# A decoder step on one core: closing one mLSTM head in a later list, opening the next in an earlier one

## Chip, cores and metric

One Trainium2 chip, one core of it. The metric is the device time of one execution in microseconds (us). Of the kernel before, three runs were timed: 988.92, 989.26 and 992.3; their median is 989.26.

## What is computed

One inference step of a two-layer decoder, in fp32, for one prompt of 512 tokens and eight samples of one new token each, which share the weights. Layer 0 is a sparse attention (compressed, selected and window branch), layer 1 an mLSTM with four heads of width 512; each mixer has one input and one output projection. The change touches the samples' part of the mLSTM. Per sample b and head, with T = 1, it is:

```
m_new = max(b + m, i);  decay = exp(b + m - m_new);  w = exp(i - m_new)
num = (q.k) w v + decay (q @ C);   den = (q.k) w + decay (q . n)
h = num / max(|den|, exp(-m_new)); h <- h * rsqrt(mean(h*h) + eps)
C <- decay C + w k v^T;            n <- decay n + w k
```

C is a 512 x 512 matrix per sample and head, 32 of them in all; each is read from HBM, used, updated and written back.

## The kernel before, in words

All tensors are laid out with features on the 128 partitions. A product in fp32 precision is made of three fp32r products: an operand x is split into xhi (a cast) and xlo = x - xhi, and hi*hi, hi*lo and lo*hi are added up in PSUM. So each weight tile is loaded by SP's DMA queue (wraw), cast by ScalarE or VectorE (whi) and subtracted by VectorE or GpSimd (wlo) before TensorE takes it.

The program is a series of seven lists of operations, numbered from 0, one after the other. A list says in which order its operations are issued; each engine takes its own operations of all lists strictly in that order. Lists 0, 1, 3 and 6 are recorded calls; lists 2, 4 and 5 are made with `P.op` and run with `P.run(ORDER, ...)` (class Plan, L485). `P.op` also notes an engine, a cost and a due time, but the class uses none of the three: the order is the tuple of operation numbers alone. ORDER1 (L108) is list 4, ORDER2 (L125) is list 5. MOVEDP1 and MOVEDP2 (L306, L310) name the operations whose first instruction goes to another engine than written (`swapped`, L651): an elementwise product, sum or difference changes between VectorE and GpSimd, a copy between ScalarE and VectorE. SLOTS (L318) gives, for each tile made, the buffer it takes; a tile waits until the last user of its buffer is done.

List 4 (L2366 to L2536) projects the 15 remaining gate columns (`zm_ops`: load, split, two chunks of 260 tokens of 24 matmuls each into mm, then zt = mm * rr, a sigmoid zsg in three ScalarE steps, the product zt * zsg, a small copy ZSS and a store zd), makes the prompt's gate rows (`gate_ops`; its last part transposes lse on TensorE and copies aT), and goes through the first sample head: state steps 0 to 7. It also issues the loads of the state tiles of steps 8 and 9.

List 5 (L2539 to L2969) is the prompt's mLSTM cell (`qk`, `v_split`, `values`), most of the output projection (`out_unit`), the samples' shares of it (`samples`) and state steps 8 to 31, that is sample heads 1 to 3. `qk` makes, per 128 features, two block diagonals bdm and bdk, the splits bh, bl of bdm and ch, cl of the input CT, and the q projection `f_po` from them.

The three pieces of a sample head:
- `head_open` (L2198). VectorE: `small`, five 128x32 products and sums into pr, wk and nT; `diag`, four copies that put q on the diagonal blocks of QZ1. TensorE: `rows`, four transposes of v. Then the split of these rows into VB, a copy (ScalarE) and a subtraction (VectorE).
- `state_step` (L2242), once per sample. TensorE: `run`, eight matmuls of two state tiles cs with QZ, kh = 1 first, into the bank d; `spread`, a broadcast of v by VB and OH. ScalarE scales the two cs tiles, VectorE adds the outer product to them, SP stores them. After the head's last step `keep` copies d to the tile ncs.
- `head_close` (L2294), a chain of nine: `small` (VectorE, tile sd), `sums` (TensorE, from ncs, sd and pr), `den` (VectorE, 3 small instructions), an absolute value (ScalarE), `num` (VectorE, 5, the last writes pr), `sq` (TensorE, from pr), `fac` (VectorE, 4), `root` (ScalarE, 2), `norm` (VectorE, 5, the last writes HN). HN of head 0 is next used by `samples` in the middle of list 5.

Before the change `state_step` calls `head_open` ahead of its head's first step and `head_close` after its last, so head 0 is opened and closed in list 4, and head 1 opened in list 5:

```
        if b == 0:                              # L2245
            head_open(P, hd, due - 8)
        ...
        if b == 7:                              # L2291
            head_close(P, hd, due + 3)
```

At the seam of the lists the orders before are, engine by engine. TensorE: last gate projection, `sq` of head 0, gate transposes; list 5: `rows` of head 1, `run` of steps 8 and 9, q projections 0 and 1, the spreads of steps 8 and 9, ... VectorE: last zt = mm * rr, `num` of head 0, last zt * zsg, `fac`, `norm`; list 5: `diag` of head 1, block diagonal 0, ... ScalarE: last sigmoid, `root`, aT; then the constant onesr; list 5: ch, ...

Of the kernel before, what the change touches and what calls it, by code (L numbers as in the profile page):

```python
# [123 lines left out]
)  # L124
ORDER2 = (  # L125
# [46 lines left out]
)  # L172
# [541 lines left out]
def step_kernel(ctx, tc, ap):  # L714
# [1527 lines left out]
    def state_step(P, k, due):  # L2242
        hd, b = divmod(k, 8)
        qz = QZ1[hd % 2]
        if b == 0:  # L2245
            head_open(P, hd, due - 8)
# [885 lines left out]
```

## Time and profile before

| | |
|---|---|
| median of three timed runs | 989.26 us (988.92 to 992.3) |
| the profiled execution, its own time | 989.0 us |
| its span, first to last instruction | 987.3 us |
| instructions | 22906 |
| mean granted TensorE clock | 0.998 of full speed |
| list 4 in the trace | from about 589 to 707 us |
| list 5 in the trace | from about 707 to 962 us |

The profile is one execution; a busy engine counts from an instruction's start to its end. Matmuls overlap in the pipeline, so from one to the next goes less time than one lasts. PE is TensorE's matmul, PEld its weight load, DVE VectorE, ACT ScalarE, POOL GpSimd, SP the queue that issues nearly all DMAs. Nearly every instruction is recorded through one helper, so rows are told apart by tile names, out<-in, and not by their line (L677).

### The profile page before, as it was taken

How to read it: one execution, taken by the hardware profiler on the slowest of the kernel's cores; microseconds unless marked ns; L12 is line 12 of the kernel's file. 1: busy time of each engine (PE TensorE's matmuls, PEld its weight loads, DVE VectorE, ACT ScalarE, POOL GpSimd, SP SyncE). 2: the span in 40 equal slices, each digit the busy share in tenths (PEclk: the TensorE clock that was granted, in tenths of full speed). 3: DMA queues.
4: the chain of work that ended last, by engine and by line, in shares of the span. 5: the costliest groups of instructions: out<-in, count | busy, mean ns of one | idle time of the engine just before them, and what ended most of it. 6: DMA issues, size and time to landing. Idle time of an engine off the chain costs nothing. (4 is left out here: it accounts for less than half of the span.)

```text
span 987.3 us, 22906 instructions
## 1 busy us (share of the span) xinstructions
PE 966.8 (98%) x8393; PEld 868.4 (88%) x8393; DVE 810.3 (82%) x1968; ACT 568.2 (58%) x1260; POOL 342.3 (35%) x418
## 2 busy tenths in 40 slices
PE   7999999999999999999999999999899999999998
PEld 5799999899988878799999997999788788778997
DVE  7988986776489988856777897966689999999986
ACT  6746443423488788633336655656687763755533
POOL 1123434421233344632133224232354633334340
PEclk9999999999999999999999999999999999999999
DMA  8755632324435434545644364887889899878643
GB/s 297 242 167 188 200 122 67 127 97 141 138 120 160 129 109 153 181 165 181 212 154 134 134 218 164 270 310 264 289 294 317 277 330 317 277 277 305 208 135 119
DMA packets 123683, 197.21 MB, mean 200 GB/s; under 512 B 16166, under 2 KB 64551, under 8 KB 123315
## 3 DMA queue, kind: packets, MB, share of 16 engines
q1 hardware_dynamic: 117954, 185.39, 57.1%
q10 hardware_dynamic: 5616, 10.36, 2.8%
q8 instruction: 66, 1.08, 0.4%
q14 instruction: 47, 0.38, 0.1%
HBM read 145.99 MB, written 58.10 MB: 207 GB/s over the span
## 5 line engine op out<-in xcount | busy, mean ns | idle before, releaser
L677 PE MATMUL mm<-hhi,whi 128*128 128x260 f32 x928 | 266.4, 287 | 0.2 <-DVE whi L677 0.2
L677 PE MATMUL mm<-hhi,wlo 128*128 128x260 f32 x928 | 262.4, 283 | 1.4 <-DVE wlo L677 1.3
L677 PE MATMUL mm<-hlo,whi 128*128 128x260 f32 x928 | 262.0, 282 | 0.0
L677 PEld LDWEIGHTS mm<-hhi,whi 128*128 128x128 f32 x928 | 174.7, 188 | 3.2 <-PE d L677 0.8
L677 PEld LDWEIGHTS mm<-hhi,wlo 128*128 128x128 f32 x928 | 174.8, 188 | 2.1 <-DVE wlo L677 2.0
L677 PEld LDWEIGHTS mm<-hlo,whi 128*128 128x128 f32 x928 | 174.7, 188 | 1.1 <-issue 0.5
L677 POOL TENSOR_TENSOR wlo<-wraw,whi 128x512 fp32r<-128x512 f32 (+1 forms) x35 | 64.4, 1842 | 121.9 <-DVE whi L677 43.1
L677 DVE SCALAR_TENSOR_TENSOR cs<-t,wk,cs 128x512 f32<-128x512 f32 x128 | 88.7, 742 | 11.2 <-ACT cs L677 10.4
L677 DVE TENSOR_TENSOR wlo<-wraw,whi 128x1024 fp32r<-128x1024 f32 (+1 forms) x64 | 73.9, 1155 | 10.4 <-ACT whi L677 6.5
L677 ACT ACTIVATE cs<-cs,SBC 128x1024 f32<-128x1024 f32 x64 | 71.3, 1146 | 12.5 <-PE d L677 10.4
L677 ACT ACTIVATE s<-s,mn 128x256 f32<-128x256 f32 (+3 forms) x128 | 70.6, 555 | 7.6 <-DVE mn L677 4.9
L677 ACT ACTIVATE whi<-wraw 128x1024 fp32r<-128x1024 f32 (+1 forms) x59 | 51.2, 871 | 41.1 <-PE mm L677 26.7
L677 POOL TENSOR_SCALAR s<-s,sm 128x256 f32<-128x256 f32 (+3 forms) x53 | 50.6, 965 | 53.9 <-DVE sm L677 27.1
L677 PE MATMUL mm<-uh,whi 128*128 128x260 f32 x224 | 65.0, 290 | 1.8 <-DVE kwl L677 1.8
L677 PE MATMUL mm<-uh,wlo 128*128 128x260 f32 x224 | 63.6, 284 | 0.3 <-POOL wlo L677 0.3
L677 PE MATMUL mm<-ul,whi 128*128 128x260 f32 x224 | 63.3, 283 | 0.3 <-DVE ul L677 0.3
L677 DVE CUSTOM_DVE_ANT_0 s<-s,D 128x128 f32<-128x128 f32 (+3 forms) x128 | 58.3, 485 | 5.5 <-PE s L677 4.1
L677 PE MATMUL s<-phi,w1a 128*128 128x256 f32 (+1 forms) x224 | 49.1, 297 | 0.0
L677 PE MATMUL mm<-uo,whi 128*128 128x260 f32 x256 | 46.2, 283 | 0.0
L677 PEld LDWEIGHTS mm<-uh,whi 128*128 128x128 f32 x224 | 42.1, 188 | 3.8 <-DVE kwl L677 2.0
L677 DVE TENSOR_TENSOR plo<-praw,phi 128x256 fp32r<-128x256 f32 (+1 forms) x50 | 39.1, 792 | 7.1 <-ACT phi L677 4.0
L677 PEld LDWEIGHTS mm<-ul,whi 128*128 128x128 f32 x224 | 42.2, 188 | 1.3 <-issue 0.5
(526 smaller groups left out, 2648.1 us busy)
## 6 DMA issues: line engine op xcount, KB each, us to landing
cs<-in_state_C SPq DMA_DIRECT2D x64, 512.0 KB, 5.5
o_cs<-cs SPq DMA_DIRECT2D x64, 512.0 KB, 5.0
praw<-in_cache SPq DMA_DIRECT2D x128, 128.0 KB, 3.1
dk<-in_cache SPq DMA_DIRECT2D x128, 128.0 KB, 2.6
wraw<-in_m_in SPq DMA_DIRECT2D x32, 512.0 KB, 4.2
wraw<-in_m_out SPq DMA_DIRECT2D x32, 256.0 KB, 4.6
wraw<-in_w_kv SPq DMA_DIRECT2D x11, 512.0 KB, 5.0
wraw<-in_w_q SPq DMA_DIRECT2D x8, 512.0 KB, 3.3
```

Source lines behind the costliest of these rows:

```text
L677: return f(*[real(x) for x in a], **{n: real(x) for n, x in k.items()})
```

## The change

Head 0 is closed in list 5 instead of list 4 (its operations are now the first that list 5 makes), and head 1 is opened in list 4 instead of list 5. List 4 has 344 operations instead of 348, list 5 has 1033 instead of 1029. No operation is added or dropped in total, and none of the moved ones issues a DMA. ORDER1 and ORDER2 are new throughout, and so are MOVEDP1, MOVEDP2 and the buffers in SLOTS from list 4 on. The code, and the first of the two swap lists:

```diff
@@ -304,16 +305,16 @@
     850, 855, 860, 870, 899, 906, 916, 920, 921, 922, 923, 924, 927, 928, 929, 930, 933,
 )
 MOVEDP1 = (
-    1, 12, 16, 22, 27, 31, 32, 46, 57, 61, 62, 72, 77, 82, 87, 91, 92, 102, 107, 112, 117, 121, 132, 136, 137, 142,
-    147, 151, 166, 172, 177, 182, 187, 192, 196, 197, 202, 212, 225, 230, 244, 248, 255, 328,
+    1, 12, 16, 17, 32, 42, 46, 47, 62, 77, 87, 91, 92, 97, 102, 117, 121, 127, 136, 151, 157, 162, 166, 177, 181,
+    182, 192, 196, 197, 202, 222, 225, 230, 342,
 )
 MOVEDP2 = (
-    75, 82, 170, 265, 272, 287, 288, 291, 292, 294, 309, 313, 325, 327, 328, 330, 331, 348, 349, 351, 353, 371, 376,
-    386, 401, 413, 423, 425, 426, 427, 433, 436, 438, 443, 451, 454, 459, 475, 476, 477, 483, 490, 493, 494, 495,
-    501, 515, 520, 525, 537, 545, 556, 557, 561, 565, 571, 575, 576, 579, 583, 585, 600, 601, 605, 609, 616, 618,
-    619, 621, 623, 631, 634, 637, 642, 666, 691, 699, 707, 725, 731, 741, 748, 772, 774, 776, 778, 781, 784, 786,
-    793, 794, 795, 808, 811, 813, 814, 817, 823, 824, 826, 828, 835, 838, 845, 851, 858, 864, 865, 871, 879, 900,
-    920, 925, 926, 933, 937, 941, 951, 959, 977, 999, 1006, 1020,
+    79, 86, 174, 269, 276, 287, 289, 291, 293, 295, 307, 313, 314, 321, 331, 335, 349, 350, 352, 353, 355, 361, 366,
+    367, 375, 379, 380, 385, 390, 397, 421, 431, 432, 433, 434, 436, 439, 458, 463, 476, 478, 487, 493, 497, 499,
+    510, 519, 524, 534, 561, 565, 571, 572, 574, 577, 578, 580, 581, 586, 587, 589, 592, 595, 601, 602, 605, 607,
+    619, 620, 623, 625, 627, 637, 640, 641, 643, 646, 649, 671, 695, 703, 711, 719, 729, 730, 734, 752, 760, 771,
+    774, 785, 786, 787, 790, 792, 794, 797, 798, 799, 802, 806, 815, 828, 839, 840, 842, 844, 845, 849, 855, 861,
+    862, 869, 882, 889, 903, 904, 929, 937, 945, 955, 963, 1003, 1010, 1024,
 )
 SLOTS = {
     ("wstream", "w"): (
@@ -2242,7 +2243,7 @@
     def state_step(P, k, due):
         hd, b = divmod(k, 8)
         qz = QZ1[hd % 2]
-        if b == 0:
+        if b == 0 and hd != 1:
             head_open(P, hd, due - 8)
         for n in (2 * k, 2 * k + 1):
             if ("cs", n) not in D:
@@ -2533,6 +2534,7 @@
     for n in range(2 * NZ, 2 * NZ + 4):
         state_load(P, n, ZT * 15 - 10)
         D["cs", n].users.append(-1)
+    head_open(P, 1, ZT * 15 - 8)
     P.run(ORDER1, R, NE, MOVEDP1)
     r1.close()
     wctx.close()
@@ -2946,6 +2948,9 @@
     P = Plan({**CAPS, "bdk": 5, "bdm": 2, "ctw": 2, "qf": 2, "qh": 2, "ql": 2, "ch": 2, "cl": 2, "bh": 2, "bl": 2, "kwh": 1, "kwl": 1, "cpt": 2, "wb": 1, "zs": 1, "ab": 1, "wt": 2,
               "Sh": 1, "Sl": 1, "acc": 1, "sq1": 1, "hx": 1, "hy": 1, "fraw": FWB[0], "fhi": FWB[1], "flo": FWB[2]},
              held + CTI + sum(VTI, []), KEPT)
+    for n in (("nc", 0), ("pr", 0), ("pr", 1), ("wk", 1)):
+        D[n] = Tile_(n[0])
+    head_close(P, 0, 0)
     for k in range(NZ, 32):
         state_step(P, k, CS0 + CSP * (k - NZ))
     v_split(P, 0, 0)
...
```

The orders at the seam after the change, engine by engine (a star: on the other engine by the swap lists):
- TensorE, list 4: `rows` of head 1 between the projections of column 12; at the end the last gate projection, gate transposes. List 5: `sums` of head 0, spreads of steps 8 and 9, q projection 0, `run` of steps 8 and 9, q projections 1 and 2, the scores of tiles 0 and 1, q projection 3, the scores of tile 2, `sq` of head 0, `run` of step 10, ...
- VectorE, list 4: `diag` of head 1 before the first zt of column 13, VB by two instructions behind it; at the end the first zt of column 15, the second gate product of column 14, `keep` of head 0, the last zt = mm * rr, aT. List 5: block diagonals 3* and 1*, `small` of head 0, block diagonals 0* and 2*, cl 0, bl 0, bl 1, `den`, cl 1, `num`, ...; `fac` some 30 and `norm` some 70 VectorE operations later.
- ScalarE, list 4: last sigmoid. Then onesr; list 5: ch 0, bh 1, bh 0, ch 1, ...
- GpSimd, list 4: the gate product of column 15, first chunk, ZSS 14, the product of its second chunk*, ZSS 15.
- SP, list 4: store of the second tile of step 7, of the first of step 7, zd 14, load of the state tile 16 (step 8, kh = 0; before it was loaded earlier and tile 17 late), zd 15. List 5: load of tile 21, wb, load of tile 20, ab, ...

What the swap lists move, counted by kind over the whole of each list (operations, before to after):

| list 5 | written for, runs on | before | after |
|---|---|---|---|
| 512-wide differences (cl, vl, ul, wlo), products (num * zs), sums (acc) | GpSimd, on VectorE | 18 | 19 |
| the same | VectorE, on GpSimd | 28 | 24 |
| Sl (128 to 512 wide) | VectorE, on GpSimd | 9 | 8 |
| block diagonals bdm, bdk (128 wide) | GpSimd, on VectorE | 12 | 16 |
| bl (128 wide) | VectorE, on GpSimd | 11 | 10 |
| casts out of SBUF (ch, vh, whi, Sh, uh) | ScalarE, on VectorE | 16 | 19 |
| copies out of PSUM, 512 wide (qh, kwh, cpt) | ScalarE, on VectorE | 8 | 10 |
| copies, 128 wide (bh, qf) | ScalarE, on VectorE | 15 | 11 |
| nP, 4 wide | VectorE, on ScalarE | 1 | 3 |

| list 4 | written for, runs on | before | after |
|---|---|---|---|
| wlo, 1024 wide | VectorE, on GpSimd | 3 | 1 |
| wlo, 1024 wide | GpSimd, on VectorE | 6 | 7 |
| gate products, 260 wide | VectorE, on GpSimd | 16 | 12 |
| gate products, 260 wide | GpSimd, on VectorE | 2 | 1 |
| whi, 1024 wide | ScalarE, on VectorE | 11 | 10 |
| `keep`, aT and one tensor_scalar of rows | VectorE, on ScalarE or GpSimd | 3 | 0 |

## Rows read from the trace of the kernel before

**Rows 1.** The page, part 1: each engine's busy time in us, its share of the span, its instructions.
```profile
PE 966.8 (98%) x8393; PEld 868.4 (88%) x8393; DVE 810.3 (82%) x1968; ACT 568.2 (58%) x1260; POOL 342.3 (35%) x418
```

**Rows 2.** Busy time of each engine by stretch (list 4; list 5 but for its first 18 and last 12 us; its last 12). The columns are the stretch and its length, then PE, PEld, DVE, ACT and POOL busy in us with the number of instructions, the granted clock, the DMA share and GB/s.
```profile
589.00:707.00 118.00, 115.92 (x1054) 104.22 (x1052) 85.81 (x192) 71.77 (x165) 40.51 (x63) 1.00 0.75 253
...
725.00:950.00 225.00, 222.31 (x1734) 186.84 (x1733) 211.22 (x455) 135.26 (x240) 93.33 (x104) 1.00 0.86 291
950.00:962.00 12.00, 11.72 (x98) 11.51 (x97) 9.16 (x17) 5.03 (x11) 7.50 (x8) 1.00 0.01 3
```

**Rows 3.** Waits of TensorE over the whole span: what it waited for, us in total, times, the longest.
```profile
PE d L677 <- DVE QZ L677: 2.0, 1, 2.0
PE mm L677 <- DVE kwl L677: 1.8, 1, 1.8
...
PE t L677 <- DVE pr L677: 1.3, 1, 1.3
```

**Rows 4.** The same view as rows 2, in stretches of 2 us behind the seam.
```profile
708.00:710.00 2.00, 1.58 (x9) 0.71 (x13) 1.97 (x9) 2.00 (x5) 0.00 (x0) 0.68 1.05 405
710.00:712.00 2.00, 2.00 (x13) 0.34 (x5) 1.94 (x8) 1.17 (x3) 0.51 (x2) 0.50 0.99 192
```

**Rows 5.** Timeline of TensorE: start, duration, operation, out<-in, shapes, count of the merged instructions, and in brackets the idle time before and what ended it. First `sums` of head 0 in list 4, then the seam.
```profile
691.46 0.44 PE L677 MATMUL t<-sd,ncs 128*32 128x8 f32 x32
691.73 0.32 PE L677 MATMUL t<-pr,ones 128*32 128x64 f32 x8
...
703.48 0.28 PE L677 MATMUL mm<-hhi,wlo 128*128 128x260 f32 x1
705.10 0.27 PE L677 MATMUL t<-pr,ones 128*32 128x32 f32 x8 [1.33 <-DVE pr L677]
705.29 0.66 PE L677 MATMUL t<-cst,lse 128*128 128x128 f32 x4
705.79 0.60 PE L677 MATMUL t<-cst,VS 128*8 128x128 f32 x4
708.42 3.53 PE L677 MATMUL d<-cs,QZ 128*32 128x512 f32 x16 [2.03 <-DVE QZ L677]
711.88 0.61 PE L677 MATMUL mm<-ch,bh 128*128 128x512 f32 x1
...
712.79 0.40 PE L677 MATMUL mm<-ch,bh 128*128 128x512 f32 x1
...
713.49 0.62 PE L677 MATMUL t<-VB,OH 128*128 128x512 f32 x2
...
716.53 1.07 PE L677 MATMUL d<-cs,QZ 128*32 128x512 f32 x8
```

**Rows 6.** Timeline of VectorE at the seam.
```profile
701.50 0.42 DVE L677 TENSOR_TENSOR zt<-mm,rr 128x260 f32<-128x260 f32 x1
703.80 0.43 DVE L677 TENSOR_TENSOR zt<-mm,rr 128x260 f32<-128x260 f32 x1 [1.88 <-PE mm L677]
...
707.94 0.19 DVE L677 TENSOR_TENSOR HN<-nm,dn 128x32 f32<-128x32 f32 x1
708.05 0.39 DVE L677 COPY QZ<-QKS 128x8 f32<-128x8 f32 x4
```

**Rows 7.** Timeline of ScalarE at the seam.
```profile
704.71 0.87 ACT L677 ACTIVATE zsg<-zsg 128x260 f32<-128x260 f32 x2
...
707.08 0.30 ACT L677 ACTIVATE onesr<-ones 128x128 fp32r<-128x128 f32 x1
707.27 1.66 ACT L677 ACTIVATE ch<-CT 128x512 fp32r<-128x512 f32 x3
```

**Rows 8.** Timeline of SP's DMA issues before the seam.
```profile
701.64 0.33 SPq L677 DMA_DIRECT2D zd<-zt  x1
702.02 1.56 SPq L677 DMA_DIRECT2D cs<-in_state_C  x1
```

**Rows 9.** The tile view of cs over the whole span, its last line, for the loads and stores of 512 KB each.
```profile
DMA to landing us min/median/max: 3.0/5.3/9.7
```

**Rows 10.** Groups of instructions by line, engine and form between 707 and 962 us: count, busy us and mean ns of one, then the idle time before them. The first is GpSimd's, the others VectorE's.
```profile
L677 POOL TENSOR_TENSOR vl<-VT,vh 128x512 fp32r<-128x512 f32 x11 | 14.7, 1340 | 19.0 <-PE mm L677 10.8 <-DVE vh L677 6.3 <-ACT vh L677 1.9
...
L677 DVE TENSOR_TENSOR vl<-VT,vh 128x512 fp32r<-128x512 f32 x5 | 3.4, 680 | 0.0
L677 DVE CAST kwh<-t 128x512 fp32r<-128x512 f32 x5 | 3.4, 680 | 0.0
...
L677 DVE CAST vh<-VT 128x512 fp32r<-128x512 f32 x4 | 2.1, 537 | 0.0
...
L677 DVE TENSOR_TENSOR bdm<-cst,mw 128x128 f32<-128x128 f32 x5 | 1.6, 324 | 0.0
```

**Rows 11.** Timeline of all engines from 845 to 850 us.
```profile
845.92 2.53 POOL L677 TENSOR_TENSOR num<-num,zs 128x512 f32<-128x512 f32 x2
...
846.02 1.23 DVE L677 SCALAR_TENSOR_TENSOR hf_v<-rs_t,rs_y 128x8 f32<-128x8 f32 x1
...
847.28 1.19 DVE L677 TENSOR_TENSOR dn<-hf_v,dn 128x8 f32<-128x8 f32 x1
...
849.36 0.39 PE L677 MATMUL mm<-uh,whi 128*128 128x260 f32 x1 [1.78 <-DVE kwl L677]
```

**Rows 12.** The tile view of hf_v, one of the small instructions of `norm`: count, then min, median and max duration in ns.
```profile
L677 DVE SCALAR_TENSOR_TENSOR hf_v<-rs_t,rs_y x4: 166/168/1229, 707.5 to 943.1; 128x8 f32<-128x8 f32 x4
```

More of the change, by code (lines that the diff above doesn't have):

```diff
@@ L420 @@
     ("st0", "cse"): (
-        0, 1, 2, 2, 1, 0, 1, 2, 0, 1, 2, 0, 1, 0, 2, 1, 0, 2, 1, 2, 0, 2, 1, 0, 2, 1, 0, 2,
+        0, 1, 2, 1, 2, 0, 0, 1, 2, 1, 0, 2, 1, 2, 0, 2, 0, 1, 2, 0, 1, 1, 0, 2, 0, 2, 1, 0,
     ),
@@ L429 @@
     ("zp", "zsg1"): (
-        0, 1, 1, 0, 1, 0, 1, 0, 1, 0, 0, 1, 0, 1, 0, 1, 0, 1, 0, 1, 1, 0, 1, 0, 0, 1, 1, 0, 1, 0, 1, 0,
+        0, 1, 1, 0, 1, 0, 1, 0, 1, 0, 1, 0, 1, 1, 0, 1, 0, 1, 1, 0, 1, 0, 0, 1, 1, 0, 1, 0, 1, 0, 1, 0,
     ),
     ("st", "cs"): (
-        0, 1, 2, 3, 0, 1, 2, 3, 2, 1, 0, 3, 1, 0, 2, 3, 0, 2, 3, 1, 0, 3, 1, 2, 0, 3, 2, 1, 0, 2, 3, 1, 2, 0, 3, 1,
+        0, 1, 2, 3, 2, 0, 1, 3, 0, 2, 1, 3, 2, 0, 1, 3, 2, 0, 3, 1, 1, 2, 3, 0, 2, 1, 3, 0, 1, 2, 3, 0, 3, 1, 2, 0,
     ),
@@ L440 @@
     ),
[4 rows of a table added]
+    ),
     ("cella", "row"): (
[4 rows of a table removed]
-    ),
[4 rows of a table removed]
[4 rows of a table added]
+    ),
+    ("cellb", "row"): (
+        0, 1, 2, 3, 4, 5, 3, 1, 2, 0, 1, 5, 2, 3, 4, 3, 1, 5, 2, 0, 2, 3, 5, 1, 2, 4, 5, 1, 0, 3, 5, 4, 0, 1, 2, 3,
+        5, 0, 4, 1,
     ),
     ("fw", "w"): (
-        0, 1, 2, 3, 4, 5, 1, 0, 2, 3, 4, 1, 0, 5, 2, 4, 3, 1, 0, 2, 5, 4, 3, 0, 1, 3, 2, 5, 1, 0, 4, 5, 1, 2, 3, 1,
-        0, 4, 5, 2, 1, 0, 3, 2, 5, 4, 0, 3, 1, 2, 4, 5, 3, 0, 1, 4, 2, 5, 0, 3, 1, 2, 5, 4, 0, 1, 3, 4, 5, 2, 0, 3,
-        1, 2, 4, 5, 3, 0,
-    ),
-    ("cellb", "row"): (
-        0, 1, 2, 3, 4, 5, 3, 0, 2, 1, 5, 4, 0, 3, 2, 0, 4, 3, 1, 5, 3, 4, 1, 2, 3, 5, 0, 4, 1, 2, 0, 4, 1, 5, 3, 0,
-        4, 1, 2, 5,
+        0, 1, 2, 3, 4, 5, 0, 3, 4, 0, 2, 1, 5, 2, 4, 3, 1, 5, 4, 2, 0, 3, 1, 4, 3, 5, 2, 3, 4, 1, 5, 0, 2, 1, 4, 2,
+        1, 0, 4, 2, 5, 3, 1, 4, 2, 0, 2, 3, 1, 2, 0, 5, 2, 1, 4, 3, 0, 1, 5, 2, 4, 0, 1, 3, 5, 4, 2, 0, 3, 1, 5, 2,
+        4, 0, 1, 3, 5, 2,
     ),
@@ L2290, in state_step @@
             P.op("SP", 0.4, due + 5 - kh, store, r=[half[kh]], mb=0.524)
-        if b == 7:
+        if b == 7 and hd:
             head_close(P, hd, due + 3)
```

165 rows, old and new, of tables (ORDER1, ORDER2, SLOTS) are left out of this document.

## The prediction, as it was put on record

> **What bounds the kernel now.** I read the page first. TensorE is busy 98% of the span and VectorE 82% [rows 1], so a change that adds and removes no matmul can only win where TensorE waits or runs slow. Then the stages, cut at the starts of lists 4 and 5: list 4 holds 2.1 us of TensorE waiting in 118, list 5 holds 2.7 in its 225 main us and 0.3 in its last 12 [rows 2]. VectorE is busy 211.2 of those 225: it is nearly a second bound there, with 13.8 us to spare. Then who was waited for: the three longest single waits outside the start of the program are for QZ (2.0), kwl (1.8) and pr (1.3), all VectorE's [rows 3]. QZ and pr lie side by side at the seam of the two lists. There the granted clock also falls to 0.68 and 0.50 [rows 4], that is to the lower level, 1.2 GHz.
>
> **The seam before, step by step** [rows 5]. Call z the end of list 4's last projection matmul, 703.48 + 0.28 = 703.76. TensorE then has the first head's closing sums of squares (start 705.10), gate transposes (705.29), the second head's opening transposes (705.79), two state steps (708.42) and list 5's first q projection (711.88, the next starts 712.79). Undisturbed these take 0.2 + 0.5 + 0.6 + 2.1 (twice the 1.07 of the step at 716.53) + 0.7 (713.49 - 712.79) = 4.1. They took 712.79 - 703.76 = 9.0, so 4.9 was lost: 1.3 waiting for pr, 2.0 for QZ, 1.5 at the lower clock. The cause is VectorE's order. pr is a link of the closing's chain, and the opening's copies into QZ (708.05) are queued behind the chain's last link at 707.94, though they need nothing of it [rows 6]. ScalarE is held too: its first work for list 5 starts at 707.08, though the last sigmoid ended at 704.71 + 0.87 = 705.6; the closing's root stands between [rows 7].
>
> **What the change does there.** Opening the second head in list 4 makes QZ, the transposes and VB ready before z: TensorE's 0.6 of transposes goes before z, beside projections it would do anyway, and VectorE's part (about 2 us) lies in list 4, where VectorE idles 118 - 85.8 = 32 us [rows 2]. Neither step issues a DMA. After z TensorE's new order is: gate transposes, closing sums, two spreads, q projection, two state steps.
> - The sums need sd, behind the last zt product, the aT copy and two block diagonals on VectorE. The product ends at z + 0.5 (703.80 + 0.43 [rows 6]); 0.2 + 2 x 0.32 + 0.2 [rows 10, 12] put sd at z + 1.5. The transposes end at z + 0.5, so TensorE waits 1.0. This is the wait that replaces the one for pr.
> - Sums 0.6 (691.46 to 691.73 + 0.32), spreads 0.5: z + 2.6 [rows 5].
> - The projection needs ch, cl, bh, bl. ScalarE: last sigmoid to z + 1.8, onesr, ch at z + 2.0 to 2.6 [rows 7]; VectorE: cl 0.7 (as the vl subtraction [rows 10]), bl 0.2, ready at z + 3.5. TensorE waits 0.9 more, then projects to z + 4.2 and steps to z + 6.3.
> Lost: 1.9 instead of 4.9, if the clock holds. I take it that it does: the wait of 1.78 before 849.36 [rows 11] falls in a stretch that stayed at the full clock [rows 2], and the two new waits are 1.0 and 0.9 with matmuls between. Gain: **3.0**. Bounds: no more than 4.9; at worst the clock falls all the same (1.5) and the state tile of step 8 lands late. That load is now the last of list 4 on SP's queue, behind a zd store that waits for a gate product placed after the product of 701.50. That product ends at z - 1.8 [rows 6], the gate product some 0.4 later, and SP issues the load 0.4 behind the store [rows 8]: at about z - 1.0. Loads of this kind land after 3.0 / 5.3 / 9.7 us (least, median, most) [rows 9], this one then at z + 2.0 / 4.3 / 8.7, and step 8 needs it for its second half at z + 4.7: nothing lost at the median, 4.0 at the most. So the seam gives between -2.5 and +4.9.
>
> **The rest of list 5.** I counted, per kind, the operations that the two swap lists move, after minus before. From GpSimd to VectorE: five 512-wide subtractions or products (0.68 [rows 10]), one narrower (at most 0.68), five 128-wide (0.32): 5.7 us. From ScalarE: three net casts out of SBUF (0.54), two out of PSUM (0.68), less four 128-wide (at most 0.32) and two tiny ones: 1.4. The closing brings 18 small instructions of 0.17 [rows 12], 3.1; the opening takes away 1.9. VectorE has **about 8 us more** in list 5; GpSimd has at least 6 x 1.34 = 8.0 less [rows 10]. The 8 lie beside TensorE's work as long as the 13.8 of VectorE's idle time covers them; without that cover they would be TensorE's waits.
> Against this stands what GpSimd costs VectorE: two closing instructions of 0.17 took 1.23 and 1.19 while GpSimd ran two products (845.92, 2.53), and TensorE's wait of 1.78 for kwl is queued behind them [rows 11, 12].
> The trace has no row for the new order. From both sides: the change can return no more than the 2.7 + 0.3 that TensorE waits there [rows 2], and loses no more than all 8 us. I take **+0.7**: that one wait of 1.8 needs a coincidence of GpSimd and a chain, likelier gone than not with GpSimd relieved, while other small waits will come up with VectorE at 97%.
>
> **A rule on the pages.** The row shows small VectorE instructions of two inputs held for about as long as a GpSimd product lasts [rows 11]. The Trainium skill, GPSIMD Engine Reference, Specifications, says that GpSimd shares its SBUF interfaces with VectorE and contends with its instructions of two SBUF inputs or in a two-port mode. The trace agrees with that. It speaks against moving the closing into list 5. As a mechanism here: GpSimd's busy share rises from 40.5/118 to 93.3/225 around the moved chain [rows 2], and a chain held as at 846 costs 2.1 us of VectorE more. With the 8 that makes 10, still under 13.8, so the sum stays and rival C gets a larger chance.
>
> **The sum.** 3.0 + 0.7 = 3.7 off the profiled execution's 989.0 (span 987.3 and 1.7 around it) gives 985.3; the median of the runs shown stands 0.3 higher: **985.6**. List 4's other moves I cost at nothing: some 6 us more for VectorE, covered by its 32 idle.
>
> **Rivals.**
> A, everything goes: the seam as worked out or better, and list 5's waits vanish. For: those waits are few and one place holds most of them; against: VectorE gets fuller. 989.3 - 3.0 - 3.0 = 983.3, at best 989.3 - 4.9 - 3.0 = 981.4. Chance 0.25.
> B, the gap only changes its owner: the state tile lands late and the clock falls, 4.0 + 1.5 more than I forecast: 989.3 - 3.0 + 5.5 = 991.8. It decides from a landing later than 5.7 us after issue. For: the range of landings; against: the median. Chance 0.15.
> C, the other side: VectorE becomes list 5's bound. Place: 725 to 950; price: the 8 us, or 10 with held chains; it decides when VectorE's added work exceeds what its idle time, spread as it lies, can take. 989.3 - 3.0 + 8 = 994.3, up to 996.3. For: 94% busy already; against: 13.8 idle and less GpSimd. Chance 0.10.
> That the change doesn't do what it says (VectorE held as often as before) lies in the forecast's lower edge: 986.3 without the 0.7.
>
> **Numbers.** The forecast's own case, 984 to 988, has 0.50. A measurement here can tell about 0.5%, 4.9 us: below 984.3 is faster, above 994.2 slower. Faster: nearly all of A and a fifth of the forecast, 0.34. Slower: half of C and the tail of B, 0.07. Same: 0.59. Range 982.0 to 991.5: it leaves out A's best, the costlier half of B, and C.
>
> **What would show it.** Right: no wait for QZ or pr at the seam; one wait near 1.0 for sd or nc before the closing sums and one below 1 for the first projection; full clock from 700 to 715; state steps 8 and 9 done by z + 6.5; VectorE's busy time in list 5 up by some 8, GpSimd's down by as much. Wrong: a wait for a DMA of cs at the seam (B), VectorE without idle time and TensorE waiting for ql, kwl or bl through list 5 (C), or the lower clock still granted there.

## The result, and the profile after

The changed kernel takes **984.18 us** (median of 5 runs, 983.27 to 984.77) against 989.53 (5 runs) beside it: a ratio of 0.9941, 95% interval 0.9929 to 0.9952, so 5.3 us or 0.6% less. 985.6 was forecast, with a range of 982.0 to 991.5. The profiled execution took 984.77, its span is 983.0.

The page's first line after [rows 1]: VectorE is a little busier (810.3 to 812.5), GpSimd less (342.3 to 326.0), TensorE the same within 0.7.

```profile
PE 966.1 (98%) x8393; PEld 868.3 (88%) x8393; DVE 812.5 (83%) x1986; ACT 568.0 (58%) x1260; POOL 326.0 (33%) x400
```

The gain is found by cutting both traces at three events of TensorE: the first state step of list 4, z (the start of list 4's last projection matmul plus 0.28), the first score product (`s<-qh,ch`), and the first matmul of the closing phase (`s<-uh,whi`). Below I call the stretches list 4, the seam and the rest. Stage windows, columns as in [rows 2]; the kernel before:

```profile
604.80:703.76 98.96, 98.96 (x841) 91.69 (x840) 70.75 (x123) 59.92 (x116) 32.27 (x43) 1.00 0.80 272
703.76:714.64 10.88, 7.51 (x44) 4.11 (x44) 8.03 (x35) 7.39 (x18) 2.60 (x6) 0.84 0.98 303
714.64:947.44 232.80, 230.11 (x1778) 193.09 (x1777) 218.87 (x473) 145.61 (x259) 97.05 (x111) 1.00 0.86 289
```

and the changed kernel:

```profile
605.75:704.78 99.03, 99.00 (x807) 91.64 (x807) 76.40 (x137) 61.06 (x116) 19.83 (x33) 1.00 0.79 277
704.78:712.12 7.34, 6.03 (x72) 3.14 (x70) 6.04 (x23) 6.71 (x17) 2.68 (x7) 1.00 0.67 201
712.12:943.24 231.12, 230.27 (x1786) 193.13 (x1785) 219.06 (x487) 144.93 (x260) 91.78 (x100) 1.00 0.87 294
```

List 4 takes the same (98.96, 99.03). The **seam** goes from 10.88 to 7.34, 3.5 less, though it now holds 72 matmuls instead of 44 (the closing's first sums came in; the opening's transposes and the closing's sums of squares went out, which cost TensorE about as much). The **rest** goes from 232.80 to 231.12, 1.7 less, and TensorE's idle time in it from 2.69 to 0.85 (the stretch less PE's busy time in the rows above). Together, with list 4's 0.07, 5.15. The spans differ by 4.2 only, since in this execution list 4 began 0.95 later (605.75 for 604.80).

TensorE's timeline at the seam, which answers to [rows 5]; z is 704.50 + 0.28 = 704.78:

```profile
704.50 0.28 PE L678 MATMUL mm<-hhi,wlo 128*128 128x260 f32 x1
704.62 0.60 PE L678 MATMUL t<-cst,lse 128*128 128x128 f32 x4
705.96 0.44 PE L678 MATMUL t<-sd,ncs 128*32 128x8 f32 x32 [0.74 <-DVE sd L678]
...
706.49 0.73 PE L678 MATMUL t<-VB,OH 128*128 128x512 f32 x2
707.78 0.49 PE L678 MATMUL mm<-ch,bh 128*128 128x512 f32 x1 [0.56 <-ACT bh L678]
...
708.76 1.93 PE L678 MATMUL d<-cs,QZ 128*32 128x512 f32 x16
...
712.12 0.39 PE L678 MATMUL s<-qh,ch 128*128 128x512 f32 x1
```

TensorE's waits over the whole span. QZ, kwl and pr [rows 3] are gone from the list, and these three have come up in lists 4 and 5:

```profile
PE t L678 <- DVE sd L678: 0.7, 1, 0.7
...
PE t L678 <- DVE cwn L678: 0.6, 1, 0.6
PE mm L678 <- ACT bh L678: 0.6, 1, 0.6
```

The granted clock stays at its upper level where it was 0.68 and 0.50 [rows 4], and its mean over the span is 1.000 in all five timed executions (0.998 in the profiled one of the kernel before):

```profile
708.00:710.00 2.00, 2.00 (x15) 0.79 (x18) 1.87 (x10) 2.00 (x7) 0.10 (x1) 1.00 0.74 160
710.00:712.00 2.00, 2.00 (x14) 1.15 (x7) 1.94 (x6) 1.94 (x5) 1.18 (x3) 1.00 0.90 280
```

VectorE's and SP's timelines at the seam [rows 6, 8]:

```profile
704.82 0.43 DVE L678 TENSOR_TENSOR zt<-mm,rr 128x260 f32<-128x260 f32 x1 [1.20 <-PE mm L678]
705.26 0.17 DVE L678 COPY aT<-t 128x16 f32<-128x16 f32 x1
...
705.75 0.16 DVE L678 TENSOR_TENSOR sd<-cst,SBC 128x8 f32<-128x8 f32 x1
```

```profile
703.48 0.43 SPq L678 DMA_DIRECT2D cs<-in_state_C  x1
```

VectorE now goes from the last product to the aT copy and on to sd without waiting for a sigmoid, since the last gate product was given to GpSimd.

### The profile page after: what moved, and what is told of

Read it like the earlier page. It is cut to its first block, busy times and chain, and to the rows that moved or that the text cites. A ratio compares the mean times of both kernels' runs of the same rounds, so it can differ in the third digit from the quotient of the medians.

```text
span 983.0 us, 22909 instructions
## 1 busy us (share of the span) xinstructions
PE 966.1 (98%) x8393; PEld 868.3 (88%) x8393; DVE 812.5 (83%) x1986; ACT 568.0 (58%) x1260; POOL 326.0 (33%) x400
## 4 chain that ended last, share of the span: by engine, by line
PE 89%; DVE 5%; ACT 2%; DMA 2%; issue 1%; POOL 0%; ACTq 0%; DVEq 0%; POOLq 0%; SPq 0%
PE mm L678 57%; PE s L678 13%; PE t L678 13%; PE d L678 6%; DMA wraw<-in_m_out 1%; DMA x_t<-in_xT 1%; DVE wlo L678 1%; DVE num L678 0%; DVE cs L678 0%; DVE plo L678 0%; DMA wraw<-in_w_kv 0%; ACT zsg L678 0%; DVE ctw L678 0%; DVE w1a L678 0%; DVE s L678 0%
## 5 line engine op out<-in xcount | busy, mean ns | idle before, releaser
L678 DVE TENSOR_TENSOR wlo<-wraw,whi 128x1024 fp32r<-128x1024 f32 (+1 forms) x68 | 77.0, 1133 | 10.5 <-ACT whi L678 7.1
L678 POOL TENSOR_TENSOR wlo<-wraw,whi 128x512 fp32r<-128x512 f32 (+1 forms) x31 | 55.6, 1793 | 89.2 <-DVE whi L678 33.0
```

The source lines that it names most:

```text
L678: return f(*[real(x) for x in a], **{n: real(x) for n, x in k.items()})
```

## The experiments

Two theories stood at the start. **S**, the prediction's: the two head moves relieve the seam and that is most of the gain. **L**: the new orders and engine choices of list 5 give it, and the head moves little. Each kernel was timed in 5 to 12 runs, the change beside 5 runs of the kernel before and the others beside 20 or 29; the median of the kernel before in those three later series was 990.3 to 990.6, so ratios are compared, not medians of different series. The stretches are those above, of the one profiled execution. A star marks a seam that holds another set of matmuls than the changed kernel's.

| kernel | median us | ratio, 95% interval | list 4 | seam | rest |
|---|---|---|---|---|---|
| before | 989.5 | 1 | 98.96 | 10.88* | 232.80 |
| the change | 984.18 | 0.9941, 0.9929 to 0.9952 | 99.03 | 7.34 | 231.12 |
| both_moved | 990.08 | 0.9994, 0.9985 to 1.0002 | 99.84 | 8.42 | 233.94 |
| open_only | 991.54 | 1.0014, 1.0004 to 1.0024 | 101.47 | 9.47* | 232.75 |
| close_only | 990.04 | 0.9989, 0.9980 to 0.9998 | 98.25 | 9.96* | 233.99 |
| new4 | 989.47 | 0.9988, 0.9978 to 0.9998 | 99.11 | 8.38 | 233.89 |
| new5 | 986.44 | 0.9955, 0.9942 to 0.9968 | 99.77 | 9.41 | 231.34 |
| old_engines | 1009.73 | 1.0194, 1.0179 to 1.0208 | 99.03 | 7.83 | 253.59 |
| new_engines | 1014.18 | 1.0231, 1.0208 to 1.0255 | 99.14 | 9.36 | 258.89 |
| fill_qz | 988.63 | 0.9980, 0.9969 to 0.9991 | 98.98 | 9.42* | 233.43 |
| products_on_vector | 988.56 | 0.9979, 0.9964 to 0.9993 | 98.98 | 11.90* | 231.14 |
| new4_products | 988.69 | 0.9983, 0.9967 to 1.0000 | 99.14 | 8.36 | 232.86 |
| steps_first | 985.67 | 0.9947, 0.9928 to 0.9966 | 99.40 | 8.24 | 230.75 |
| steps_first_early | 984.53 | 0.9934, 0.9913 to 0.9955 | 99.03 | 6.96 | 232.20 |

**both_moved: the head moves alone.** Buffers and banks are handed out as in the kernel before; the moved steps stand at places that I chose.

```diff
 list 4, before's order
-closing of head 0
+small hd1 (early); rows, diag, VB copy behind the spread of step 6; VB subtraction behind a ft13 projection
 list 5, before's order
-opening of head 1
+sd and sums hd0 first; den behind the first bl; num behind the third cl; sq, fac, root, norm before the first use of HN
```

> The kernel before with the closing of head 0 and the opening of head 1 moved as in the change; every other step of lists 4 and 5 keeps its place and its engine. Theory S (the seam: the head moves remove the waits for pr and QZ and keep the full clock, and the rest of list 5 gives the rest): 3.0 to 3.5 us off, about 986.2, no wait for pr or QZ, granted clock 1.00 from 700 to 715, and the wait of 1.8 for kwl near 849 still there. Rival L (the new orders and engine choices of list 5 give it, the head moves little): no more than 1 us off, 988.5 or above.

S fell as to the sum: 0.6 us off, within the noise. The waits for pr and QZ are gone, the clock stays at 1.00 at the seam and the seam is 2.5 shorter, but two new waits stand in it (for sd and for a state tile), and the kernel loses 0.9 in list 4 (my place for the VB subtraction, ahead of a whi cast, makes TensorE wait 0.9 for wlo) and 1.1 in the rest (a second wait for kwl, 0.8, near 735). The wait for sd is 1.98 instead of 0.74, because VectorE's last gate product, which waits for the last sigmoid, stands ahead of sd. VectorE's timeline, then TensorE's:

```profile
704.85 0.43 DVE L677 TENSOR_TENSOR zt<-mm,rr 128x260 f32<-128x260 f32 x1 [1.88 <-PE mm L677]
706.67 0.43 DVE L677 TENSOR_TENSOR zt<-zt,zsg 128x260 f32<-128x260 f32 x1 [1.39 <-ACT zsg L677]
707.01 0.16 DVE L677 TENSOR_TENSOR sd<-cst,SBC 128x8 f32<-128x8 f32 x1
```

```profile
707.23 0.44 PE L677 MATMUL t<-sd,ncs 128*32 128x8 f32 x32 [1.98 <-DVE sd L677]
...
708.60 1.92 PE L677 MATMUL d<-cs,QZ 128*32 128x512 f32 x16 [0.78 <-DMA cs<-in_state_C]
```

So the moves alone put other waits in the place of the old ones. The clock also fell in a second place, behind the wait of 1.8 for kwl near 849. The kernel before has the same wait [rows 11] and stayed at 1.00 behind it. Stage windows, the kernel before, then both_moved:

```profile
850.00:852.00 2.00, 2.00 (x15) 1.86 (x15) 1.72 (x4) 1.56 (x3) 1.31 (x1) 1.00 0.26 94
```

```profile
850.00:852.00 2.00, 2.00 (x12) 2.00 (x11) 1.13 (x3) 0.76 (x2) 1.28 (x1) 0.53 0.39 145
852.00:854.00 2.00, 2.00 (x9) 1.71 (x8) 1.62 (x5) 2.00 (x5) 0.00 (x0) 0.62 0.98 271
```

Matmul by matmul, that fall put TensorE 1.4 further behind the kernel before, but it had this back by 883, where small waits that the kernel before has fell away. The clock fell behind the same wait in close_only and new4 too (0.50 in 852 to 854), but not in fill_qz and open_only.

**open_only and close_only: one move each.**

```diff
 open_only:  list 4 +opening of head 1 (as above), closing stays;  list 5 -opening
 close_only: list 4 -closing of head 0;  list 5 +closing (as above), opening stays
```

> The kernel before with only the opening of head 1 moved into list 4; the closing stays in list 4. Theory S: the wait for QZ (2.0) goes and with it the lower clock (1.5); the wait for pr (1.3) stays: 2.5 to 3.5 us off, about 986.5. If the clock falls after the wait for pr alone, 2.0 off. Rival L: no more than 0.5 us off.

> The kernel before with only the closing of head 0 moved into list 5; the opening stays in list 5. Theory S: the wait for pr (1.3) goes, a wait for QZ or for the closing's sd stays, since the opening's copies and sd are now both first in list 5's VectorE queue: 1 to 2 us off without the clock, 3 with it; about 988. Rival L: within 0.5 us of the kernel before.

open_only is slower, and part of that is my own: the bank that its transposes got was still waiting for ScalarE's copy of the first head's products to ncs (first row), 1.9 in list 4. That total decides nothing. Its seam does: QZ is no longer waited for, yet after the wait for pr TensorE waits 0.88 for a state tile, and the clock falls to 0.82 and 0.50 in 710 to 714.

```profile
687.98 0.60 PE L677 MATMUL t<-cst,VS 128*8 128x128 f32 x4 [1.89 <-ACT ncs L677]
...
709.36 0.27 PE L677 MATMUL t<-pr,ones 128*32 128x32 f32 x8 [1.33 <-DVE pr L677]
...
711.09 3.52 PE L677 MATMUL d<-cs,QZ 128*32 128x512 f32 x16 [0.88 <-DMA cs<-in_state_C]
```

close_only comes out 1.1 us faster, at the near end of what S said: pr is gone, sd takes its place with 2.07, and the clock falls to 0.50 in 708 to 710 (the 16 matmuls of the two steps take 3.02, against 1.93 in the change).

```profile
707.07 0.41 PE L678 MATMUL t<-sd,ncs 128*32 128x8 f32 x29 [2.07 <-DVE sd L678]
...
708.92 3.02 PE L678 MATMUL d<-cs,QZ 128*32 128x512 f32 x16 [0.46 <-DMA cs<-in_state_C]
```

**new5 and new4: one list of the change at a time.** Both have the head moves.

```diff
 new5: ORDER1, MOVEDP1 as both_moved;  ORDER2, MOVEDP2 as the change
 new4: ORDER1, MOVEDP1 as the change;  ORDER2, MOVEDP2 as both_moved
```

> List 5 as in the change, list 4 in the order and with the engine choices of the kernel before (only the two head moves made in it). Theory S: list 4's new order is worth nothing, so 5.0 to 5.4 us off, about 984.3, as the change itself. Rival L says the same of this run. A second rival, that list 4's new order matters for the seam (the state tile's load, the last products), loses 1 us or more of it: 985.5 or above.

> List 4 as in the change, list 5 in the order and with the engine choices of the kernel before (only the two head moves made in it). Theory S: the seam's part alone, 3.0 to 3.5 us off, about 986.2, and the wait for kwl near 849 is still there. Rival L: no more than 1 us off.

With both_moved and the change these make a square. List 5's order with its engine choices is worth 0.39% over list 4 of both_moved (0.9994 to 0.9955) and 0.47% over the change's (0.9988 to 0.9941), 3.9 to 4.7 us; list 4's is worth 0.06% to 0.14%, 0.6 to 1.4 us, each difference with an uncertainty of about 0.15%, so list 4's can't be told from nothing. **L is right about the place in the program**: the head moves give little alone, and list 5's order with its engine choices gives most. Whether the head moves are needed isn't shown: no kernel here has list 5's new order without them, and fill_qz and products_on_vector below, which move neither head, each gain about 2 us. In the profiled executions 2.6 to 2.8 of list 5's part is the rest (233.9 to 231.2). From new4 to the change another 1.0 lies at the seam; from both_moved to new5 the seam of the profiled executions grew by 1.0, so there the place of the remainder isn't shown. new4 also shows that clearing VectorE's end of list 4, as the change does by giving the last gate product to GpSimd, isn't enough by itself: sd is waited for 0.43 only, yet the seam is 8.38, since the steps directly behind the sums take 2.7 and the q projections wait for bh and bl.

```profile
706.61 2.79 PE L677 MATMUL d<-cs,QZ 128*32 128x512 f32 x16
...
711.18 0.50 PE L677 MATMUL mm<-ch,bh 128*128 128x512 f32 x1 [0.49 <-ACT bh L677]
```

new5 came out on the side of its second rival (985.5 or above), though its ratio can't be told from the change's: its list 4 costs 0.7 and its wait for sd is 2.38. In three of its other four executions the mean clock is 1.000, but in the profiled one (988.0, 1.6 above its median) the clock then fell:

```profile
708.00:710.00 2.00, 1.67 (x42) 1.40 (x43) 1.97 (x9) 1.89 (x6) 0.05 (x1) 0.56 1.06 312
710.00:712.00 2.00, 2.00 (x8) 0.89 (x11) 1.86 (x9) 1.33 (x5) 0.00 (x0) 0.59 0.90 297
```

In new4 the rest keeps kwl's waits:

```profile
PE mm L677 <- DVE kwl L677: 2.6, 2, 1.8
```

**products_on_vector: what held kwl.**

```diff
 MOVEDP2 of before
+555, 563   # the num * zs products at 845.92 and 847.19: GpSimd -> VectorE
```

> The kernel before with the two num products that GpSimd does at 845.92 (2.53 us) given to VectorE, behind the kwl subtraction in its queue. If GpSimd's products hold the two small closing instructions: hf_v and dn take 0.17 each, kwl comes 2.1 us earlier, the wait of 1.78 is gone and 1.7 us come off, about 987.8. Rival (the wait is VectorE's queue): the wait stays and the time is the same, or longer by the 1.4 us that the products take on VectorE.

The hold is GpSimd's. Both small instructions take 0.17 instead of 1.23 and 1.19 [rows 11], kwl follows at once, and TensorE doesn't wait for it. VectorE's timeline:

```profile
848.41 0.17 DVE L677 SCALAR_TENSOR_TENSOR hf_v<-rs_t,rs_y 128x8 f32<-128x8 f32 x1
848.62 0.17 DVE L677 TENSOR_TENSOR dn<-hf_v,dn 128x8 f32<-128x8 f32 x1
...
848.93 0.68 DVE L677 TENSOR_TENSOR kwl<-t,kwh 128x512 fp32r<-128x512 f32 x1
```

The rest is 1.66 shorter, about as much as the wait of 1.78; the ratio says 2.1 us, 0.7 to 3.6. (The seam is 1.0 longer in this execution: the clock stayed at its lower level until about 715 instead of 712.) The 1.4 us of added work on VectorE cost nothing that can be seen. new4_products asks whether this adds to new4:

```diff
 new4's MOVEDP2
+the same two products
```

> As new4, and the two num products near 846 are given to VectorE behind kwl. If the parts add: new4's 1.2 us and the products' 1.7 make 2.9 off, the main stretch falls from 233.9 to about 232.1, and what is left to the changed kernel is list 5's other order. If they don't add (another wait takes the place of kwl's): 1.2 to 2 off.

The rest shrinks by 1.0, not 1.7, and the ratio lies between the two answers with an interval that holds both: inconclusive. Its seam shows the tile wait again:

```profile
707.21 1.91 PE L677 MATMUL d<-cs,QZ 128*32 128x512 f32 x12 [1.14 <-DMA cs<-in_state_C]
```

**fill_qz: does idle time bring the lower clock?**

```diff
 rows(), head 1 (list 5 of before)
+dm = xb()
+for n in range(16): PE.transpose(dm[0:8, n % 4 * 128:(n % 4 + 1) * 128], vs[:, n % 4], ident)
```

> The kernel before with 16 more transposes of 128x8 behind the opening's four, into a bank that nobody reads, so that TensorE works through most of the wait of 2.0 for QZ. The wait's end is VectorE's and stays. If TensorE's idle time brings the lower clock: the granted clock stays 1.00 from 708 to 712 and 1.5 us come off, about 988.0. Rival (the clock falls for another reason, as the DMA load): same time as before, 0.68 and 0.50 again.

Yes, at this seam. With the wait filled, VectorE's QZ comes no sooner, but the steps run at full clock: 16 matmuls from 708.81 to 710.73 instead of 708.42 to 711.88 [rows 5].

```profile
706.18 2.35 PE L678 MATMUL t<-cst,VS 128*8 128x128 f32 x20
708.81 1.99 PE L678 MATMUL d<-cs,QZ 128*32 128x512 f32 x16 [0.28 <-DVE QZ L678]
```

```profile
708.00:710.00 2.00, 1.72 (x17) 0.80 (x19) 1.90 (x11) 2.00 (x5) 0.00 (x0) 1.00 0.79 239
710.00:712.00 2.00, 2.00 (x14) 1.05 (x7) 1.94 (x6) 1.83 (x6) 0.47 (x1) 1.00 1.03 267
```

The seam is 1.46 shorter; 0.6 of that is given back in the rest, for which no run here shows the cause. The ratio says 2.0 us, 0.9 to 3.1. The other executions agree: the mean clock is 1.000 in 8 of the 12 timed runs of fill_qz, and in 4 of the 78 of the kernel before in the three series.

**old_engines and new_engines: order and engine choices apart.**

```diff
 old_engines: the change;  MOVEDP2 -> before's choices, by operation
 new_engines: new4;        MOVEDP2 -> the change's choices, by operation
```

> The changed kernel with the order of both lists kept and list 5's engine choices (the swap list) put back to those of the kernel before. Theory S: the seam's 3.0 to 3.5 us stay; of the remaining 1.9 some or all is lost, as GpSimd gets its products back: 984.3 to 986.2. Rival L: most of the 5.3 us is lost, 987.5 or above.

> As new4 (list 4 as in the change, list 5 in the order of before with the two head moves), but with the changed kernel's engine choices in list 5. If the engine choices alone relieve VectorE of GpSimd: the main stretch falls from 233.9 to about 231.3 and the kernel is 4 to 5 us faster than before. If order and choices only work together: slower than before, as the changed order with the old choices was (1.9%).

Neither order works with the other's choices: 1.9% and 2.3% slower. In old_engines TensorE waits for GpSimd's acc and VectorE's ql, in new_engines for VectorE's results all through list 5. TensorE's waits, first of old_engines:

```profile
PE t L677 <- POOL acc L677: 5.0, 1, 5.0
...
PE s L677 <- DVE ql L677: 2.7, 2, 2.1
```

and of new_engines:

```profile
PE mm L677 <- DVE kwl L677: 3.8, 3, 2.5
PE mm L677 <- DVE cl L677: 3.8, 1, 3.8
```

So "GpSimd relieved" is no gain by itself: in new_engines VectorE's instructions were held for 25 us in all, against 11 in new4 (the excess over the lower quartile of each kind of instruction, summed where it is more than 0.05), with less work on GpSimd. The clock has a share in both times: its mean in the profiled executions is 0.996 and 0.993, with 0.50 in 762 to 766 of old_engines and four such places in new_engines.

**steps_first and steps_first_early: a better seam?**

```diff
 list 5 of the change
-PE: sums hd0, spread 8, spread 9, projection, steps 8 and 9
+PE: spread 8, spread 9, steps 8 and 9, sums hd0, projection
 steps_first_early, list 4 too
+load of tile 16 directly behind the load of tile 19
```

> The changed kernel, with TensorE's spreads and state steps 8 and 9 ahead of the closing sums in list 5, to fill the waits of 0.7 (sd) and 0.6 (bh) at the seam. If only those waits count: 0.6 to 1.3 us faster than the changed kernel, about 6.5 to 7 off the kernel before. Rival: the steps now want state tile 16, whose load is issued at 703.5 in the changed kernel and lands 5.4 to 6.1 later: TensorE waits for it until about 709.2, 3 us, the clock falls, and the kernel is 1 to 4 us slower than the changed one.

> As steps_first, and the load of state tile 16 is issued right behind that of tile 19, some 5 us earlier, so that it has landed. If the seam's two waits count: 0.6 to 1.3 us faster than the changed kernel, no wait above 0.3 at the seam. Rival: the first scores then wait for ql instead (it ends at 711.6 in the changed kernel): the same time as the changed kernel, 5.3 to 5.9 off.

In steps_first the tile is waited for, as the rival said, but 0.63, not 3, and the clock held at 1.00 until 716; its ratio can't be told from the change's.

```profile
712.63 0.64 PE L677 MATMUL d<-cs,QZ 128*32 128x512 f32 x4 [0.63 <-DMA cs<-in_state_C]
```

The profiled execution of steps_first (990.6) is the slowest of nine. It lost that time where the two kernels are the same, ahead of list 4, which began 5.0 later than in the change.

With the early load the wait for the tile is gone, and the rival of steps_first_early comes in: the projections wait for cl and bh instead.

```profile
709.41 0.50 PE L677 MATMUL mm<-cl,bh 128*128 128x512 f32 x1 [0.57 <-DVE cl L677]
...
710.55 0.50 PE L677 MATMUL mm<-ch,bh 128*128 128x512 f32 x1 [0.41 <-ACT bh L677]
```

Its seam is 0.4 shorter, its rest 1.1 longer: 0.9934 against 0.9941, no difference that can be told. No kernel here is faster than the change by more than the noise.

## Why the prediction was right, and where it was not

**The seam: right, a little small.** Forecast 3.0, measured 3.5. Each step came some 0.3 to 0.5 early against z: sd ready at z + 1.1 (z + 1.5 forecast; the two block diagonals overlap and take 0.48 together, not 0.64), the projection at z + 3.0 (z + 3.5), the steps' end at z + 5.9 (z + 6.3). The two waits are 0.74 and 0.56 instead of 1.0 and 0.9, and the second is ended by ScalarE's bh, not by VectorE's cl and bl as the prediction had it. That the clock would hold was right, and fill_qz shows that the idle time in front of the steps had lowered it. One of the two reasons given was luck: the wait of 1.78 for kwl that the prediction saw pass at full clock was followed by the lower clock in both_moved, close_only and new4. The prediction read the gain off the changed order and never asked which edit gave it. both_moved answers: the two moves alone take 2.5 off the seam and give 2.0 of it back in list 4 and the rest.

**The state tile: right, with less to spare than it looked.** Its load is issued at 703.48, z - 1.3 (z - 1.0 forecast), and isn't waited for. In six other kernels a state tile is waited for at the seam, for 0.46 to 1.14. So rival B's mechanism is real, but none of these waits came near its price of 4.0. What shields the change is the work in front of its steps, the sums and the projection: steps_first, which puts the steps ahead of both, waits 0.63 for the tile, and with the earlier load of steps_first_early that wait is gone.

**The rest: the right sign, the term mis-sized.** Forecast +0.7, measured 1.7. The one wait that the prediction named, kwl's, is gone, and products_on_vector shows that its cause was the one named. What was mis-sized is the small waits: the prediction took 1.8 for kwl's and took 1.1 off again for others that would come up "with VectorE at 97%". Of the new waits only cwn's 0.65 is longer than 0.25, TensorE's idle time in the rest fell by 1.84, and products_on_vector, without the other edits, has nearly the same 1.66.

The 97% rested on the step "VectorE has about 8 us more in list 5", and that isn't what came. From z to the closing phase VectorE is busy 8.03 + 218.87 = 226.9 before and 6.04 + 219.06 = 225.1 after. Two things were left out. Of the closing's 18 instructions 14, 2.4 us, lay after z in the kernel before too, so about 5.6 was to be expected from z on. And VectorE's instructions are held less: the excess over the lower quartile of their kind, summed as above, falls from 13.4 to 6.6. With the holds taken out, the summed durations grow by 4.5 us, near the 5.6. On GpSimd the same sum without holds falls by about 9 (at least 8.0 forecast), its busy time in these stretches by 5.2. So the count of work was fair; what failed is that it left the holds as they were. That the lighter GpSimd alone did this isn't shown: new_engines has it too, and 25 us of holds.

**The rule on the pages.** The moved chain was held once, and TensorE paid: hf_v took 1.22 instead of 0.17 beside a GpSimd subtraction, ctw stood behind it, and TensorE waited 0.65 for ctw's sum cwn. Timeline of the changed kernel:

```profile
721.08 3.05 POOL L678 TENSOR_TENSOR vl<-VT,vh 128x512 fp32r<-128x512 f32 x2
...
721.16 1.22 DVE L678 TENSOR_SCALAR hf_v<-hf_v 128x8 f32<-128x8 f32 x1
...
722.30 0.68 DVE L678 CUSTOM_DVE_ANT_0 ctw<-CT,wb 128x512 f32<-128x512 f32 x1
...
723.04 1.16 PE L678 MATMUL t<-bdk,ctw 128*128 128x128 f32 x8 [0.65 <-DVE cwn L678]
```

The prediction took this as a possible 2.1 us of VectorE under cover; one hold of 1.05 cost 0.65. The Trainium skill, GPSIMD Engine Reference, Specifications, names two SBUF inputs or a two-port mode as the condition; this instruction has one tensor input, and no run here shows its mode.

**The rivals.** A came nearest (983.3 against 984.18; the forecast of 985.6 is 1.4 off). C did not come in the change, but waits for VectorE all through list 5 are what new_engines shows (with GpSimd's acc in old_engines), at 19 to 24 us and not at 8, part of it the clock's. So the 13.8 us of idle time that the prediction counted as cover don't suffice for these choices in every order.

**List 4 at nothing**: right, 98.96 to 99.03.

## What to carry to other kernels

When a wait is caused by a queue, look at all that stands ahead of the waiting step: in both_moved a product that waits for a sigmoid took the old wait's place, and in new4, without it, the next operands did. Here an order and its engine choices went only together; a count of work by engine told what fits, not what it costs in another order. Count what the clock may lose behind a long wait of TensorE, look for it in several executions and not in one, and test it by filling the wait with matmuls that nobody reads.

## What was not expected

The length of the wait alone doesn't tell whether the clock falls. At the seam the profiled execution of both_moved waited 1.98 and stayed at 1.00; waits of 2.03 (before), 2.07 (close_only) and 2.38 (new5) were followed by 0.50 to 0.56 in the lowest stretch of 2 us, though not in every execution of new5; in open_only two waits of 1.33 and 0.88, with 0.9 of short matmuls between, were followed by 0.50. Near 850 a wait of 1.8 was followed by the lower clock in three kernels and not in three others. The transposes that kept it up in fill_qz are 128x8 products that nobody reads.

The holds on VectorE were long for their instructions: three of 8 elements per partition took 1.19 to 1.23 instead of 0.17, beside GpSimd instructions of 512 that took about 1.3 to 1.5.
